# Sliding windows by DMA alone: from two DMA rings to three, with larger copy and store pieces and one more staged batch

## The chip, the cores and the metric

The kernel runs on one core of one Trainium2 chip. The metric is the device time of one execution in microseconds, given as the median of several runs; a profiled execution is taken besides, and all details come from it. The kernel does no arithmetic. It consists of DMA transfers, which the core's 16 DMA engines carry out, and of waits on semaphores.

## The reference

The input `x` has 32 batches of 4096 rows with 256 float32 numbers, 4 MiB a batch. The output takes windows of 64 rows, with a step of 32 rows, so 127 windows a batch, each a plain copy:

```
for i in range(n_windows):            # 127
    start = i * stride                # stride 32
    result[:, i] = x[:, start:start + window_size].copy()   # window 64
```

A window is 64 KB and two neighbours share half of their rows. So nearly every input row is written twice, and the output has 266 MB against an input of 134 MB.

## The kernel before, in words

A batch is seen as 128 blocks of 32 rows (32 KB each). Window w is block w followed by block w + 1. Output batches come about in two ways.

**Copied batches** (20 of 32) go straight from the input to the output in DRAM. `copy` (L93) issues three transfers on the SP queue, of 80, 32 and 15 windows (`COPY_PARTS`, L16). The second number there is how many pieces a 64 KB window is cut into: 16 KB, 32 KB and 16 KB a piece. A piece becomes one DMA packet. Copied data is read twice from the input, since neighbouring windows overlap.

**Staged batches** (12 of 32: 1, 3, ..., 23; `STAGED`, L9) are read once. `load` (L75) brings a batch into one of five tiles in the on-chip memory (`BUFS`, L10), a block on each of 128 partitions. `store` (L83) writes the tile out twice: once as the first halves of the windows, once as the second halves. Both are on the ACT queue, in pieces of 16 KB. Each store covers 128 half windows where a batch has only 127 windows, so the last first-half falls into the next batch's first window, and the first second-half into the previous batch's last window. These halves are garbage there.

So the neighbours of a staged batch must be written after its stores. The order of the copies on SP (`_order`, L102) is this: four `EARLY` batches (L12), which are copied first of all and whose damaged halves are written again at the end (L152 to L158, seven transfers of one 32 KB half each); then batches with no staged neighbour, and the others spread among them, each placed well behind the stores that it waits for (`after_store`, L71, called at L137).

On ACT the order is written out by hand: load 0, load 1, the stores of batch 0, load 2, the stores of batch 1, and so on (L139 to L148). A load into a tile that was used before waits for that tile's stores (L79). At the end SP waits for all stores and copies and clears twelve semaphores one by one (L159 to L163).

Every transfer is issued in `start` (L62), so all DMA lines of the profile carry L62. A queue's transfers lie in a ring per DMA engine; when the ring is full, the issuing instruction lasts until there is room.

Of the kernel before, what the change touches and what calls it, by code (L numbers as in the profile page):

```python
# [1 line left out]

# [4 lines left out]


STAGED = tuple(range(1, 24, 2))  # L9
BUFS = 5  # L10

EARLY = (18, 20, 22, 24)  # L12

BLOCK_PARTS = 2

COPY_PARTS = ((80, 4), (32, 2), (15, 4))  # L16


class _Geometry:


    def __init__(self, x, out, W, S):
        self.B, self.L, self.D = x.shape
        self.x, self.out = x, out
        self.n_win = (self.L - W) // S + 1
        self.n_blk = self.L // S
        self.blk = S * self.D
        self.win = W * self.D
        assert W == 2 * S and self.n_blk == self.n_win + 1 == 128

    def src(self, b, block, dims):

        at = (b * self.n_blk + block) * self.blk
        return bass.AP(self.x.tensor, self.x.offset + at, dims)

    def dst(self, b, half, dims):

        at = b * self.n_win * self.win + half * self.blk
        return bass.AP(self.out.tensor, self.out.offset + at, dims)

    def rows(self, b, w0, n):

        s, d = [[self.blk, n], [1, self.win]], [[self.win, n], [1, self.win]]
        return self.dst(b, 2 * w0, d), self.src(b, w0, s)

    def half(self, b, half, block):

        dims = [[self.blk // 16, 16], [1, self.blk // 16]]
        return self.dst(b, half, dims), self.src(b, block, dims)


class _Kernel:
    def __init__(self, nc, g, tiles):
        self.nc, self.g, self.tiles = nc, g, tiles
        self.loaded = [nc.alloc_semaphore(f"loaded{i}") for i in range(len(tiles))]
        self.stored = [nc.alloc_semaphore(f"stored{i}") for i in range(len(tiles))]
        self.copied = nc.alloc_semaphore("copied")
        self.early = nc.alloc_semaphore("early")
        self.count = {}

    def start(self, engine, out, in_, sem, parts=1):
        engine.dma_start(out=out, in_=in_, max_dma_last_dim=65536 // parts).then_inc(sem, 16)  # L62
        self.count[id(sem)] = self.count.get(id(sem), 0) + 16

    def all_of(self, engine, sem):
        engine.wait_ge(sem, self.count[id(sem)])

    def slot(self, n):
        return divmod(n, len(self.tiles))

    def after_store(self, engine, n):  # L71
        turn, i = self.slot(n)
        engine.wait_ge(self.stored[i], 32 * (turn + 1))

    def load(self, n):  # L75

        g, (_, i) = self.g, self.slot(n)
        if n >= len(self.tiles):
            self.after_store(self.nc.scalar, n - len(self.tiles))  # L79
        src = g.src(STAGED[n], 0, [[g.blk, g.n_blk], [1, g.blk]])  # L80
        self.start(self.nc.scalar, self.tiles[i][:, :], src, self.loaded[i], 2 * BLOCK_PARTS)

    def store(self, n):  # L83

        g, (turn, i) = self.g, self.slot(n)
        self.nc.scalar.wait_ge(self.loaded[i], 16 * (turn + 1))
        for half in (0, -1):
            dst = g.dst(STAGED[n], half, [[g.win, g.n_blk], [1, g.blk]])  # L90
            self.start(self.nc.scalar, dst, self.tiles[i][:, :], self.stored[i], 2 * BLOCK_PARTS)

    def copy(self, b, sem):  # L93

        w = 0
        for rows, parts in COPY_PARTS:
            self.start(self.nc.sync, *self.g.rows(b, w, rows), sem, parts)
            w += rows
        assert w == self.g.n_win


def _order(B):  # L102


    near = {b for s in STAGED for b in (s - 1, s + 1)}
    order = list(EARLY) + [b for b in range(B) if b not in near and b not in STAGED]
    tied = sorted(near - set(EARLY))
    n = len(order) + len(tied)
    for b in tied:
        behind = max(STAGED.index(s) for s in (b - 1, b + 1) if s in STAGED)  # L110
        order.insert(-(-(2 * behind + 5) * n // (2 * len(STAGED))), b)
    return order


@with_exitstack
def kernel(
    ctx: ExitStack,
    tc: tile.TileContext,
    x: bass.AP,
    window_size: bass.AP,  # L120
    stride: bass.AP,
    out: bass.AP,
):
    nc = tc.nc
    W, S = int(window_size), int(stride)
    g = _Geometry(x, out, W, S)
    assert 0 not in STAGED and g.B - 1 not in STAGED
    pool = ctx.enter_context(tc.tile_pool(name="blocks", bufs=1))
    tiles = [pool.tile([g.n_blk, g.blk], x.dtype, name=f"xb{i}") for i in range(BUFS)]

    with tc.tile_critical():
        k = _Kernel(nc, g, tiles)
        for b in _order(g.B):
            if b not in EARLY:
                for s in (b - 1, b + 1):
                    if s in STAGED:
                        k.after_store(nc.sync, STAGED.index(s))  # L137
            k.copy(b, k.early if b in EARLY else k.copied)
        k.load(0)  # L139
        waited = False  # L140
        last = len(STAGED) - 1
        for n, s in enumerate(STAGED):
            if n < last:
                k.load(n + 1)
            if not waited and (s - 1 in EARLY or s + 1 in EARLY):
                k.all_of(nc.scalar, k.early)
                waited = True
            k.store(n)  # L148


        k.all_of(nc.sync, k.early)
        for n, s in enumerate(STAGED):  # L152
            if s - 1 in EARLY or s + 1 in EARLY:
                k.after_store(nc.sync, n)
            if s - 1 in EARLY:
                k.start(nc.sync, *g.half(s - 1, 2 * g.n_win - 1, g.n_blk - 1), k.copied)
            if s + 1 in EARLY:
                k.start(nc.sync, *g.half(s + 1, 0, 0), k.copied)  # L158
        for n in range(len(STAGED)):  # L159
            k.after_store(nc.sync, n)  # L160
        k.all_of(nc.sync, k.copied)
        for sem in [*k.loaded, *k.stored, k.copied, k.early]:
            nc.sync.sem_clear(sem)  # L163


# [1 line left out]
_INS = ['x', 'window_size', 'stride']  # L167
_OUTS = [((32, 127, 64, 256), 'float32')]

_NUMBERS = {'window_size': 64, 'stride': 32}  # L170


# [26 lines left out]
```

## Time and profile before

| | us |
|---|---|
| median of 3 runs (lowest to highest) | 767.51 (767.38 to 767.76) |
| the profiled execution | 768.4 |
| its span, first to last instruction | 766.6 |
| first DMA packet starts, last one ends (from the span's start) | 2.0, 763.8 |
| SP's issue of a copy's three transfers, median from issue to landing | 114.8, 116.7, 97.7 |
| ACT's load, ACT's store, median from issue to landing | 123.2, 84.6 |

The page of this kernel has nothing under the compute engines: GpSimd sets four constants at the start. What counts are the slices of part 2 (busy share of the DMA engines and the rate that they moved data at), the queues of part 3 (q1 is SP's, q10 is ACT's), and the answers on stretches of the span. A row of such an answer gives the stretch, its length, GpSimd's busy time, the clock of the matrix engine (of no matter here), the busy share of the DMA engines and the GB/s.

The long times from issue to landing are time in the ring, behind other transfers.

### The profile page before, as it was taken

How to read it: one execution, taken by the hardware profiler on the slowest of the kernel's cores; microseconds unless marked ns; L12 is line 12 of the kernel's file. 1: busy time of each engine (PE TensorE's matmuls, PEld its weight loads, DVE VectorE, ACT ScalarE, POOL GpSimd, SP SyncE). 2: the span in 40 equal slices, each digit the busy share in tenths (PEclk: the TensorE clock that was granted, in tenths of full speed). 3: DMA queues.
4: the chain of work that ended last, by engine and by line, in shares of the span. 5: the costliest groups of instructions: out<-in, count | busy, mean ns of one | idle time of the engine just before them, and what ended most of it. 6: DMA issues, size and time to landing. Idle time of an engine off the chain costs nothing. (4 is left out here: it accounts for less than half of the span.)

```text
span 766.6 us, 180 instructions
## 1 busy us (share of the span) xinstructions
POOL 0.2 (0%) x4
## 2 busy tenths in 40 slices
POOL 0000000000000000000000000000000000000000
DMA  8999999999999999999999999999999999999996
GB/s 371 425 410 421 405 428 431 408 411 427 423 415 421 431 415 425 432 408 416 427 420 417 431 420 420 423 428 410 414 427 419 422 428 418 417 428 421 420 406 237
DMA packets 19837, 317.70 MB, mean 414 GB/s; under 512 B 1628, under 2 KB 1628, under 8 KB 1740
## 3 DMA queue, kind: packets, MB, share of 16 engines
q1 hardware_dynamic: 10044, 166.70, 51.9%
q10 hardware_dynamic: 9792, 151.00, 47.3%
q14 instruction: 1, 0.01, 0.0%
HBM read 217.02 MB, written 267.35 MB: 632 GB/s over the span
## 5 line engine op out<-in xcount | busy, mean ns | idle before, releaser
L180 POOL MEMSET const-bfloat16-1.0<- 128x1 bf16 x1 | 0.1, 102 | 0.0
L180 POOL MEMSET const-uint8-127<- 128x1 uint8 x1 | 0.1, 102 | 0.0
L180 POOL MEMSET const-float32-0.0<- 128x1 f32 x1 | 0.1, 99 | 0.2 <-issue 0.2
L180 POOL MEMSET const-float32-1.0<- 128x1 f32 x1 | 0.1, 99 | 0.0
## 6 DMA issues: line engine op xcount, KB each, us to landing
out_dram<-in_x_dram SPq DMA_DIRECT2D x20, 5120.0 KB, 114.8
out_dram<-xb ACTq DMA_DIRECT2D x24, 4096.0 KB, 84.6
xb<-in_x_dram ACTq DMA_DIRECT2D x12, 4096.0 KB, 123.2
out_dram<-in_x_dram SPq DMA_DIRECT2D x20, 2048.0 KB, 116.7
out_dram<-in_x_dram SPq DMA_DIRECT2D x20, 960.0 KB, 97.7
out_dram<-in_x_dram SPq DMA_DIRECT2D x7, 32.0 KB, 48.3
```

The costliest lines, as they stand in the source:

```text
L180: nc = _bacc.Bacc("TRN2", target_bir_lowering=False, num_devices=1)
```

## The change

- `STAGED` gets a 13th batch (25), and `EARLY` moves up by two, to 20, 22, 24, 26. There are 19 copied batches left.
- Copies stay on SP. A batch is now two transfers: 112 windows in pieces of 64 KB, and 15 windows in pieces of 16 KB for the first 12 copies, 32 KB for the last 7.
- Stores stay on ACT, in pieces of 32 KB.
- Loads 1 to 12 move to the GpSimd queue, in pieces of 16 KB as before. There they are issued one after the other, the first four without a wait.
- The first load is split by columns into two halves, the first transfer of SP and of ACT, with a semaphore of its own.
- At the end GpSimd, not SP, waits for everything, resets its DMA queue, and clears all semaphores in one instruction.

```
-STAGED = tuple(range(1, 24, 2))
+STAGED = tuple(range(1, 26, 2))
-EARLY = (18, 20, 22, 24)
-BLOCK_PARTS = 2
-COPY_PARTS = ((80, 4), (32, 2), (15, 4))
+EARLY = (20, 22, 24, 26)
+LOAD_PARTS = 2
+REST_PARTS = (4, 2)
+FIRST_COPIES = 12
...
     def load(self, n):
-            self.after_store(self.nc.scalar, n - len(self.tiles))
+            self.after_store(self.nc.gpsimd, n - len(self.tiles))
-        self.start(self.nc.scalar, self.tiles[i][:, :], src, self.loaded[i], 2 * BLOCK_PARTS)
+        self.start(self.nc.gpsimd, self.tiles[i][:, :], src, self.loaded[i], 2 * LOAD_PARTS)
+    def load_first(self):
+        g, n = self.g, self.g.blk // 2
+        for j, engine in enumerate((self.nc.sync, self.nc.scalar)):
+            at = g.src(STAGED[0], 0, [[g.blk, g.n_blk], [1, g.blk]])
+            src = bass.AP(at.tensor, at.offset + j * n, [[g.blk, g.n_blk], [1, n]])
+            self.start(engine, self.tiles[0][:, j * n : (j + 1) * n], src, self.first)
...
     def store(self, n):
-        self.nc.scalar.wait_ge(self.loaded[i], 16 * (turn + 1))
+        if n == 0:
+            self.all_of(self.nc.scalar, self.first)
+        else:
+            self.nc.scalar.wait_ge(self.loaded[i], 16 * (turn + (i > 0)))
         for half in (0, -1):
-            self.start(self.nc.scalar, dst, self.tiles[i][:, :], self.stored[i], 2 * BLOCK_PARTS)
+            self.start(self.nc.scalar, dst, self.tiles[i][:, :], self.stored[i])
-    def copy(self, b, sem):
-        for rows, parts in COPY_PARTS:
-            self.start(self.nc.sync, *self.g.rows(b, w, rows), sem, parts)
+    def copy(self, b, sem, rest_parts):
+        whole = self.g.n_win // 16 * 16
+        self.start(self.nc.sync, *self.g.rows(b, 0, whole), sem)
+        self.start(self.nc.sync, *self.g.rows(b, whole, self.g.n_win - whole), sem, rest_parts)
...
+        k.load_first()
+        for c, b in enumerate(_order(g.B)):
...
+            k.copy(b, k.early if b in EARLY else k.copied, REST_PARTS[c >= FIRST_COPIES])
-        k.load(0)
+        for n in range(1, len(STAGED)):
+            k.load(n)
...
         for n in range(len(STAGED)):
-            k.after_store(nc.sync, n)
-        k.all_of(nc.sync, k.copied)
-        for sem in [*k.loaded, *k.stored, k.copied, k.early]:
-            nc.sync.sem_clear(sem)
+            k.after_store(nc.gpsimd, n)
+        for sem in [*k.loaded, k.first, k.early, k.copied]:
+            k.all_of(nc.gpsimd, sem)
+        nc.gpsimd.dma_reset()
+        used = sorted(sem.num for sem in [*k.loaded, *k.stored, k.first, k.early, k.copied])
+        assert used == list(range(used[0], used[-1] + 1))
+        nc.gpsimd.sem_clear(range(used[0], used[-1] + 1))
```

## The prediction

> **What bounds the kernel now.** No compute engine works here, so the chain of waits is empty and I read the page's slices, then its queues, then the rates in stretches, and last the wait list.
>
> ```profile
> span 766.6 us, 180 instructions
> ...
> DMA  8999999999999999999999999999999999999996
> GB/s 371 425 410 421 405 428 431 408 411 427 423 415 421 431 415 425 432 408 416 427 420 417 431 420 420 423 428 410 414 427 419 422 428 418 417 428 421 420 406 237
> DMA packets 19837, 317.70 MB, mean 414 GB/s; under 512 B 1628, under 2 KB 1628, under 8 KB 1740
> ## 3 DMA queue, kind: packets, MB, share of 16 engines
> q1 hardware_dynamic: 10044, 166.70, 51.9%
> q10 hardware_dynamic: 9792, 151.00, 47.3%
> ...
> HBM read 217.02 MB, written 267.35 MB: 632 GB/s over the span
> ```
>
> The 16 DMA engines are busy from the second slice to the end (51.9% + 47.3% of their span). So time is work on the engines, and only three things move it: bytes, what a byte costs, and the two ends. The second thing varies: slices go from 405 to 432 GB/s at the same busy share. The stretches of the ACT ring (q10) show when. In order: a load, the first store of a pair, the second store, a load, and so on, with copies (q1) always beside them.
>
> ```profile
> 5.00:20.00 15.00, 0.00 (x0) 1.00 1.01 433
> ...
> 84.00:105.00 21.00, 0.00 (x0) 1.00 1.00 409
> 105.00:125.00 20.00, 0.00 (x0) 1.00 1.01 431
> 125.00:146.00 21.00, 0.00 (x0) 1.00 1.01 427
> 146.00:168.00 22.00, 0.00 (x0) 1.00 1.00 398
> 168.00:188.00 20.00, 0.00 (x0) 1.00 1.02 433
> 188.00:209.00 21.00, 0.00 (x0) 1.00 0.99 420
> 209.00:232.00 23.00, 0.00 (x0) 1.00 1.01 410
> ```
>
> The last two columns are the DMA share and GB/s. Loads run at 398 to 410, first stores at 431 to 433, second stores at 420 to 427. The single packets say the same thing (counted in the trace's packet records):
>
> ```
> kind of packet        count   usual ns   mean ns
> copy 16 KB (q1)        7600        611       623
> copy 32 KB (q1)        1280       1213      1253
> load 16 KB (q10)       3072        611       650
> store 16 KB (q10)      6144        611       618
> ```
>
> 611 and 1213 differ by 602, so a packet costs 9 ns and 602 ns per 16 KB; all above that is **stall**. By the same records, stalls take 4.4% of the time of all load stretches, 0.5% of first stores, 2.2% of second stores.
>
> Now the sum of the profiled execution, for one of the 15 engines that carry most (the 15-row pieces leave one engine out, which is why the busy share falls to 0.95 from 725 to 750). A copied batch: 24 x 611 + 4 x 1213 + 27 = 19.54 us; 20 of them, 390.9. A load or store: 16 x 611 + 9 = 9.785; 36 of them, 352.3. The seven 32 KB halves: 0.7. Work 743.8. The first packet starts at 2.0, the last ends at 763.8: stalls are 18.0, which is 2.4% of the work. From there 2.9 us to the span's end: 1.1 until SP sees the last landing, 0.7 for twelve clears, 1.1 of closing barrier. 2.0 + 743.8 + 18.0 + 2.9 = 766.7, the span. The execution itself took 768.4, and the median of the runs is 767.5, 0.9 less; I apply both steps to the result.
>
> **The change, part by part.**
>
> *One more staged batch.* It adds three transfers (29.36) and takes one copied batch (19.54): +9.8 us on every engine. Nothing hides this, because the engines are the bound. In bytes: 317.7 becomes 321.9 MB.
>
> *Bigger pieces.* I take 64 KB at 4 x 602 + 9 = 2417 ns; no such packet is in the trace, so this is an estimate from the two sizes that are. If the 9 ns were charged four times, a 64 KB piece would save nothing. A copy becomes 7 x 2417 + 4 x 611 + 18 = 19.38 (with 2 x 1213 at the end 19.36): 19 of them save 3.3 us together. A store becomes 8 x 1213 + 9 = 9.71: 26 save 1.9. Loads stay at 16 x 611. New work: 368.1 (copies) + 252.5 (stores) + 127.2 (loads) + 0.7 = 748.5, so **+4.7 us net**.
>
> *Three rings.* Engines take one packet from each ring in turn: where 32 KB copies met 16 KB stores, q1's share of the bytes in 5 us pieces rose from 0.50 to between 0.6 and 0.74. So I count bytes per turn, completion packets included: copies 512 KB in 13 packets (39 KB), stores 256 KB in 9 (28), loads 256 KB in 17 (15). That is 48%, 34%, 18% of the bytes. At 431 GB/s: a copied batch per 41 us, a pair of stores per 57, a load per 54. Loads keep just ahead of stores, and 5 tiles give four loads without any wait. Store pair 12 then ends near 20 + 13 x 57 = 761 less what stores gain when loads are through (12 x 54 + 10 = 658), some 10 us; copies end near 12 x 41 + 7 x 37 = 751. The two streams finish together. SP's waits for stores cost nothing as long as its ring holds work: a batch's ring entries fall from 31 to 13, so SP issues about 2.4 times as far ahead. In the present kernel these waits show
>
> ```profile
> SPq L62 <- DMA out_dram<-xb: 61.2, 2, 40.2
> SPq L73 <- DMA out_dram<-xb: 19.2, 3, 9.4
> ```
>
> and the engines stayed full beside them; the last 40.2 is the wait of the late halves at the end.
>
> *GpSimd issues the loads.* Its queue does nothing now but four memsets. Issue time on ACT was 0.4 to 0.6 us a transfer when the ring had room; if GpSimd needs ten times that, it is still 5 of 54 us. If its loads came in smaller packets, at 4 KB say, 768 - 192 more packets x 9 ns = 5 us more work, and loads would fall behind. I take nothing and keep +5.
>
> *First load split.* Both halves lie first in both rings, so all engines load for 9.8 us and store 0 can start near 13 instead of at 43. The engines are full either way: 0 us.
>
> *Stalls.* This is what decides. 48% copies, 18% loads and 34% stores mean reads of 0.66 and writes of 0.82 bytes per byte moved, all the time. Today reads go between 0.52 (stores, stall 0.5% in the clean first ones) and 1.0 (loads, 4.4%). A straight line gives 1.6% at 0.66; if stalls rise only near full reading, it stays at 0.5%. HBM traffic per byte moved also falls, from 1.52 to 1.48. Against it stands the nearest mixture that the trace has: where the ring hands over from loads to stores or back, 2 us pieces with 1 to 35% of loads stall for **8 to 9%**.
>
> ```profile
> 146.00:152.00 6.00, 0.00 (x0) 1.00 0.99 385
> ```
>
> These are some 30 pieces of 2 us, in which engines are also out of step with each other. And with reads of 1.0, 5:20 ran at 433. So neither the read share nor the mixture alone explains a stall. The ends are 0.5% (4 us) and 8% (60 us). By composition the handover row is nearest, but it is a transient; I take the middle of the two steady rows' answers, 1.0% = 7.5 us. This is a choice more than a result.
>
> The Trainium skill speaks against this part: "DMA: Bandwidth & Descriptors", Rules for kernel authors, says that spreading DMAs over SP, ACT and GpSimd does not help bandwidth, since all run on the same 16 engines and only issue time is saved. The trace agrees that both rings share engines (the shares sum to 99%). By that rule alone the stall share stays at 2.4% and the change loses; it says nothing of the order in which reads and writes meet.
>
> *The end.* Today the halves are issued at 755.3 and 756.2, 1.9 and 2.9 us after the last store's packet (753.3), and hide behind copies that run to 763.8. Now 13 stores and 19 copies end together. If stores are last, 2.9 + 0.5 (issue) + 1.1 (issue to first packet, from the start: 0.9 to 2.0) + 0.2 is exposed: +4.7; if copies are last, 0. I take 2.4. One clear on GpSimd for twelve on SP saves 0.65; its reset of the queue is not in the trace: between 0.03 (the shortest GpSimd setup row at the start) and 1.9 (a landing round trip, above). I take 0.2. End: 2.4 us after the last landing's packet.
>
> Sum: 2.0 + 748.5 + 7.5 + 2.4 + 2.4 = 762.8 span, 764.6 as the profiled execution's time, **763.7** as a median.
>
> **Rivals.** A measurement can tell about 0.2%, 1.5 us, from no change; the forecast needs stalls below 9.8 us.
> - *Stalls level out* (forecast, stalls 3 to 9.8): 759 to 766; with the end hidden too, down to 757. For: clean store stretches at 431 to 435, HBM demand a little lower. Chance 0.53.
> - *Break-even* (1.3 to 1.7%): 766 to 769. Chance 0.12.
> - *The stall share stays at 2.4%*, because each kind of packet keeps its own: 18.0 instead of 7.5, **774.2**; slower. Place: all copies and loads, 1 to 650 us. It decides from a stall share of 1.7% on. For: loads stall 6% and copies 2%, and their shares of the bytes hardly change. With smaller load packets besides, 779. Chance 0.22.
> - *The handover state becomes the steady state*: 6 to 8% over 640 us, 38 to 51 us plus the end stretch, 797 to 811. For: the 385 row. Against: 5:20. Chance 0.13.
> - *Nothing changes in the sharing* (rings not by packet): copies then take a third, and run last, alone; that is inside the third case.
>
> **Numbers.** Faster 0.53, same 0.12, slower 0.35. The range takes in the first three cases, 757 to 780, and leaves out the fourth and a part of the third's upper end.
>
> **What would show it.** Right: three queues of 158.3, 109 and 54 MB (the first load's halves lie on SP and ACT); 64 KB packets at 2417 ns; slices without the dips of load stages, at 425 or more up to about 650 us; the last store and last copy within 10 us of each other; stalls of 1%. Wrong: loads' packets not 16 KB, slices at 420 or less throughout (third case), at 400 (fourth), or an empty stretch of the engines while SP or ACT waits.

## The result and the profile after

The change makes the kernel slower, by 1.7%: 780.36 us against 767.48, ratio 1.0169 (95% interval 1.0152 to 1.0187). The forecast was 763.7, with 780 as its upper end. The profiled execution took 780.2 us, its span is 778.4.

The page of the changed kernel, the lines that answer to those of before:

```profile
span 778.4 us, 159 instructions
...
DMA  9999999999999999999999999999999999999994
GB/s 377 418 427 423 400 418 418 444 402 446 391 444 421 436 397 435 413 427 436 411 414 428 439 409 450 392 437 422 431 414 437 398 433 412 422 411 414 414 391 190
DMA packets 11167, 321.95 MB, mean 414 GB/s; under 512 B 1341, under 2 KB 1341, under 8 KB 1453
## 3 DMA queue, kind: packets, MB, share of 16 engines
q1 hardware_dynamic: 4015, 160.47, 49.6%
q10 hardware_dynamic: 3888, 111.15, 33.6%
q0 software_dynamic: 3264, 50.33, 15.3%
HBM read 212.89 MB, written 267.42 MB: 617 GB/s over the span
```

The three queues carry what was foreseen (q0 is GpSimd's). The mean rate is the old 414 GB/s for 4.3 MB more. The slices swing harder than before. A part of that is counting, since a packet's bytes stand where it starts, so the packet records have to say what stalls.

| | before | after | forecast of after |
|---|---|---|---|
| first packet to the last one (after: to the end of the last store's) | 2.0 to 763.8 | 1.9 to 773.8 | |
| work of a busy engine, overlaps taken off | 738.9 | 745.7 | 748.5 (before 743.8) |
| stalls, mean of the engines | 19.3 | 21.3 | 7.5 |
| last engine behind that mean | 3.6 | 4.9 | 0 |
| from there to the span's end | 2.9 | 4.6 | 4.8 |

The overlaps: an engine's next packet starts about 4 ns before the record of the last one ends, which is why the DMA share reads 1.01 in places. A packet costs some 5 ns beyond its bytes, not 9. The rows differ by 6.8 + 2.0 + 1.3 + 1.7 = 11.8 us, the difference of the spans. The span is 15.6 us over its forecast of 762.8: stalls came 13.8 and the last engine 4.9 above what was forecast, work 2.8 and the two ends 0.3 below.

By kind of packet, from the same records: copies stalled 2.2% of their time before and 4.0% after (64 KB packets: 2418 ns as a rule, 2533 in the mean), loads 6.0% before and 1.4% after, stores about 1.2% in both. So the stalls did not stay with their kinds. They moved to the copies. Here is one copied batch in pieces of 4 us (shares of the bytes moved; the stall's share of all engines' time):

```
from   copies  stores  loads   stall
228      0.57    0.29   0.14   0.000
232      0.57    0.27   0.15   0.000
236      0.54    0.31   0.15   0.002
240      0.58    0.28   0.14   0.015
244      0.58    0.27   0.15   0.044
248      0.57    0.29   0.14   0.026
252      0.50    0.32   0.18   0.010
256      0.27    0.40   0.32   0.004
260      0.24    0.53   0.23   0.005
264      0.33    0.50   0.17   0.000
```

For seven packets of 64 KB the copies hold 0.57, for the four packets of 16 KB of the last 15 windows 0.25; the mean is the forecast 0.48. The stall comes late in the high stretch and is gone in the low one. Over the whole run, again in pieces of 4 us, with two kernels from below beside it (the last 40 us of each left out):

```
copies' share   changed kernel     copies in 32 KB (e4)   levelled (e5)
                pieces  stall      pieces  stall          pieces  stall
under 0.40         48   0.002         67   0.001             33   0.004
0.40 to 0.50       15   0.011         65   0.006             59   0.002
0.50 to 0.55       24   0.017         18   0.002             39   0.011
0.55 to 0.60       65   0.030          6   0.004             32   0.007
0.60 to 0.65       16   0.049          2   0.004             10   0.039
0.65 to 0.80       16   0.098          0                      8   0.060
over 0.80           0                 29   0.222              0
```

The share of the moment does not order the stalls by itself: at 0.55 to 0.60 the three kernels stall 3.0%, 0.4% and 0.7%. How long a high stretch has lasted counts too. In pieces of 2 us with a share of 0.53 to 0.65, the changed kernel stalled 1.3% in the first 6 us of a stretch (68 pieces) and 5.3% after that (80 pieces); the levelled one has 64 such early pieces, with 1.0%, and only 8 late ones, again with 5.3%.

A copied byte is read from HBM and written to HBM, so a share c of copies asks for 1 + c bytes of HBM traffic per byte moved. That made **theory A**: reads and writes together have a ceiling, and engines stall while the copies' share of the moment is over what it lets through. **Theory B**: stalls follow the HBM traffic of the whole run, so that a staged batch buys its own work back. **Theory C**: 64 KB packets stall by themselves. "HBM traffic" here is the sum of the page's two figures, read and written; no run shows whether a ceiling on it would sit in HBM or on the way there.

### The profile page after: what moved, and what is told of

It is laid out like the page before. It is cut to its first block, busy times and chain, and to the rows that moved or that the text cites. A ratio compares the mean times of both kernels' runs of the same rounds, so it can differ in the third digit from the quotient of the medians.

```text
span 778.4 us, 159 instructions
## 1 busy us (share of the span) xinstructions
POOL 8.9 (1%) x16
## 4 chain that ended last, share of the span: by engine, by line
another core or an unknown queue 64%; POOL 1%; issue 0%; PEldq 0%
POOL xb L64 1%; PEldq L208 0%
## 5 line engine op out<-in xcount | busy, mean ns | idle before, releaser
L64 POOL DMA_DIRECT2D xb<-in_x_dram x12 | 8.7, 726 | 502.4 <-DMA out_dram<-xb 501.4
```

## The experiments

**e1_twelve**, the changed kernel without the added batch:

```
-STAGED = tuple(range(1, 26, 2))
+STAGED = tuple(range(1, 24, 2))
-EARLY = (20, 22, 24, 26)
+EARLY = (18, 20, 22, 24)
```

> The changed kernel with 12 staged batches instead of 13 (EARLY back to 18, 20, 22, 24); everything else as changed. Each engine has 9.8 us less work. Theory A (an engine stalls when copies hold much of the bytes of the moment, almost not below 45%, 3% at 55 to 60%, 10% above 65%): the turns of the rings stay as they are, so stalls up to 640 us stay; copies are last and alone for some 40 us, which adds 3 to 6 us of stall but hides the late halves (3 us less). 780.4 - 9.8 + 4 - 3 = 771 to 773. Theory B (stalls follow the HBM traffic of the whole run, so that the 13th staged batch buys its own work back): 779 or more. Theory C (64 KB packets stall more by themselves): 770, with the copies' stall share unchanged at 4.6% also in the last 40 us.

Measured: 780.83 us, ratio to before 1.0167 (1.0133 to 1.0200). Work fell by 10.0 us an engine and stalls rose from 21.3 to 33.7. That is theory B's number: here the 13th batch buys its own work back. Of the stalls 22.2 us lie ahead of 640 us (16.9 in the changed kernel; the difference lies in pieces of 4 us with a share above 0.65, 21 of them with 10.0 us of stall against 10 with 4.5; in several of the 21 stores or loads moved next to nothing, and why was not settled) and 5.6 behind 738 us, where stores are through and copies run alone:

```profile
660.00:700.00 40.00, 0.00 (x0) 1.00 1.00 407
700.00:740.00 40.00, 0.00 (x0) 1.00 0.99 399
740.00:760.00 20.00, 0.00 (x0) 1.00 0.94 326
```

The last column, GB/s, drops to 326 with 15 of 16 engines at work all the time.

**e2_before13**, the added batch alone, on the kernel before (`STAGED` to 25 and `EARLY` as in the change):

> The kernel before with a 13th staged batch and nothing else of the change. Theory A: 9.8 us more work (29.36 - 19.54 per engine), a copy share that stays near 50% by the turns of two rings, stalls about as before or 1 us less; some of the late halves' wait (up to 4 us) shows at the end since stores end later: 776 to 781. Theory B: the HBM traffic falls by 4 MB in 484, and stalls by as much as the work grows: 766 to 770.

Measured: 776.92 us, ratio 1.0110 (1.0094 to 1.0126), as theory A said. Work 10.0 us more, stalls 16.8 instead of 19.3. So the added batch alone costs 1.1%, the rest of the change alone 1.7%, and both together 1.7%. On two rings theory B fails, 10.0 us of work for 2.5 us of stall; on three the batch is free. Traffic over the whole run cannot be the rule by itself.

**e3_halved**, all pieces of the changed kernel halved:

```
-LOAD_PARTS = 2
+LOAD_PARTS = 4
-REST_PARTS = (4, 2)
+REST_PARTS = (8, 4)
...
+            self.start(self.nc.scalar, dst, self.tiles[i][:, :], self.stored[i], 4)
...
+        self.start(self.nc.sync, *self.g.rows(b, 0, whole), sem, 2)
```

> The changed kernel with every piece halved: copies 32 KB (the 15 rows 8 and 16 KB), stores 16 KB, loads 8 KB; only the first load's two halves stay at 16 KB. Shares by turn stay 4 to 2 to 1, packets double. Consecutive packets overlap by about 4 ns in the trace, so a packet costs about 5 ns: 700 more packets an engine are 3.5 us. Theory A: the same shares at each moment, the same stalls: 782 to 786. Theory C: the copies' stall share falls from 4.6% to the 2 to 3% that 16 and 32 KB packets had before, 5 to 9 us less: 774 to 779.

Measured: 778.90 us, ratio 1.0141 (1.0122 to 1.0159), just inside theory C's numbers. Stalls are 18.3. By share they are as in the changed kernel at 0.55 to 0.60 (0.030) and lower above 0.65 (0.063 against 0.098). So by one profile of each the size of a packet has a part of some 3 us, where the ceiling is passed furthest; it does not remove the stalls.

**e4_copy32**, the copies alone cut smaller:

```
-REST_PARTS = (4, 2)
+REST_PARTS = (2, 2)
...
+        self.start(self.nc.sync, *self.g.rows(b, 0, whole), sem, 2)
```

> The changed kernel with copies cut to 32 KB (the 15 rows too), stores 32 KB and loads 16 KB as changed. Copies get 40% of the bytes by turn, so staged batches end early, near 635 us, and copies run the last 115 us alone. Theory A: almost no stall up to 550 us (under 1%, against 2.6% now), all of the stall at the end, where copies alone must show what they stall by themselves, 10% or more: 12 us and up; the late halves are hidden. 765 to 775, and a trace with 430 GB/s and more up to 550 us, 390 or less behind 640. Theory C: copies' stall share near 3% throughout, not piled up at the end; 770.

Measured: 792.35 us, ratio 1.0312 (1.0295 to 1.0330). Theory A had the place right and the size wrong. Its stretches:

```profile
20.00:200.00 180.00, 2.14 (x3) 1.00 1.00 429
200.00:400.00 200.00, 2.85 (x4) 1.00 1.00 433
400.00:550.00 150.00, 0.71 (x1) 1.00 1.00 432
550.00:640.00 90.00, 0.00 (x0) 1.00 1.01 429
640.00:660.00 20.00, 0.00 (x0) 1.00 1.01 341
660.00:760.00 100.00, 0.00 (x0) 1.00 0.98 326
```

For 640 us, at a copies' share of 0.4, the engines run with 3.7 us of stall in all; then copies alone stall 22% of the time at 326 GB/s, and 29.3 us of stall pile up there. The expectation had put copies alone at a stall of 10% or more, 390 GB/s or less.

**e8_copies64**, no staging at all, to measure the ceiling by itself (all 32 batches copied by SP, `COPY_PARTS = ((112, 1), (15, 1))`, no loads, stores or waits on them):

> No staging at all: SP copies all 32 batches in 64 KB pieces, everything else left out (the output is complete). It measures the ceiling by itself. Theory A: the rate is that of the end of the run with 32 KB copies, 326 GB/s, that is 652 GB/s of reads and writes: 266.3 MB take 815 us. Theory C (64 KB pieces worse than 32 KB): under 310 GB/s, over 860 us.

Measured: 817.69 us, one execution. Its page:

```profile
DMA  9999999999999999999999999999999999999996
GB/s 309 347 321 309 354 315 328 337 312 328 341 325 337 315 341 328 334 321 321 347 321 318 337 321 344 325 334 328 315 341 325 334 325 325 331 328 328 331 321 260
...
HBM read 266.34 MB, written 266.34 MB: 653 GB/s over the span
```

The engines are full from end to end and move 327 GB/s; the last line is the ceiling, **653 GB/s of reads and writes**. It is the rate of 32 KB copies alone, so 64 KB is no worse here, against theory C. With unstalled engines at 432 GB/s, 432 x (1 + c) = 653 gives c = 0.51; at 0.667 (64 KB copies beside 32 KB stores, no loads) the ceiling allows 653 / 1.667 = 392. The changed kernel's pieces above 0.65 moved about 390, and the stretch in which it ran at 0.667 steadily, with loads through, moved 396:

```profile
672.00:688.00 16.00, 0.00 (x0) 1.00 1.00 396
```

A ceiling of copies by themselves does not explain this stretch: two thirds of 396 are 264, well under the 327 that copies reach alone.

**e5_level** spreads the copies in time. Same bytes, same 13 batches, no more data packets:

```
-        whole = self.g.n_win // 16 * 16
-        self.start(self.nc.sync, *self.g.rows(b, 0, whole), sem)
-        self.start(self.nc.sync, *self.g.rows(b, whole, self.g.n_win - whole), sem, rest_parts)
+        w = 0
+        for rows, parts in ((32, 1), (32, 1), (32, 1), (16, 1), (15, 1)):
+            self.start(self.nc.sync, *self.g.rows(b, w, rows), sem, parts)
+            w += rows
```

> The changed kernel with each copied batch cut into transfers of 32, 32, 32, 16 and 15 windows, all in 64 KB pieces (before: 112 in 64 KB, 15 in smaller ones). The same bytes, 13 staged, no more packets. By turns the copies still hold 57% while they have a packet, but a completion entry now falls after every one or two packets, where it came after seven. Theory A, sharpened by the last runs (reads and writes together cannot pass about 650 GB/s for long, and a copied byte counts twice, so the copies' share must not stay above 0.5): no long stretch at 0.57 or more, stalls fall from 21 us to 10 to 16, and copies end last and hide the late halves: 765 to 773. Theory C (64 KB packets stall by themselves): the same 4.6% on copies, 778 or more.

Measured: 766.04 us, ratio 0.9997 (0.9976 to 1.0018): the loss is gone. Stalls are 11.5. Stretches of it:

```profile
200.00:400.00 200.00, 2.86 (x4) 1.00 1.01 432
400.00:640.00 240.00, 1.43 (x2) 1.00 1.00 432
640.00:740.00 100.00, 0.00 (x0) 1.00 1.00 416
740.00:754.00 14.00, 0.00 (x0) 1.00 0.96 333
```

and the same stretches of the changed kernel:

```profile
200.00:400.00 200.00, 2.86 (x4) 1.00 1.00 424
400.00:640.00 240.00, 1.43 (x2) 1.00 1.00 423
640.00:740.00 100.00, 0.00 (x0) 1.00 0.99 413
```

432 against 424 while three rings run. The copies' share by turns is that of the changed kernel's first 12 copies, 0.48: 13 ring entries for 512 KB in both. Its spread in time differs, and the last 15 windows are now 64 KB pieces, which the next run takes alone. It is not a matter of which addresses a long transfer spreads over, since e4 kept the transfers of 112 windows and hardly stalled for 640 us. What is left to lose is behind 640 us: loads are through, copies hold 0.6 and more, and from 740 they are alone.

**e10_rest64** tells whether it was the cutting or the small pieces of the 15 windows, which went as well:

```
-REST_PARTS = (4, 2)
+REST_PARTS = (1, 1)
```

> The changed kernel with one edit: the 15 windows too in 64 KB pieces, still one transfer of 112 and one of 15. It tells whether the small pieces of the 15 windows made the levelled kernel better by going, or the cutting into short transfers. Theory A: eight 64 KB packets in a row instead of seven and no low stretch between them, so the ceiling is hit more: stalls 21 us or more, 776 to 785. Rival D (the mix of sizes within a batch makes the stalls): near the levelled kernel, 766 to 770.

Measured: 782.64 us, ratio 1.0205 (1.0190 to 1.0220). So the small pieces going did not do it; that leaves the cutting. Without the low stretch between, stalls grow to 23.8; here the copies' share by turns is also higher, 0.54.

**e6_level_lead**, the second staged batch loaded at the start too (each of SP and ACT issues a half of batches 0 and 1; GpSimd starts at batch 2):

> The kernel of the run before with the second staged batch, too, loaded at the start by SP and ACT in two halves, so that loads stay a whole batch ahead and ACT need not wait for a load between two pairs of stores. Theory A: the stretches in which stores are missing and copies hold 0.65 to 0.75 go; 2 to 5 us less than the run before. If those stretches cost nothing, the same within 1 us, or up to 4 us more since loads end earlier and copies are left with stores alone for longer.

Measured: 769.49 us, ratio 1.0044 (1.0023 to 1.0064), at the upper end of its second case (about 3.5 us more than the run before). Loads were through at 586 us instead of 659, and the copies met stores alone for longer.

**e7_two32**, larger pieces on the two old rings (`BLOCK_PARTS = 1`, `COPY_PARTS = ((112, 2), (15, 2))`):

> The kernel before (two rings, 12 staged) with larger pieces alone: copies, loads and stores all in 32 KB. 560 packets an engine fewer at about 5 ns are 2.7 us less work; the copies' share by turn is 0.50 where it was 0.52. Theory A: stalls no more than before: 762 to 766. Theory C: stalls 3% and more on copies throughout, 768 to 772.

Measured: 771.50 us, ratio 1.0063 (1.0046 to 1.0081), in theory C's numbers. But the expectation had left out that staged batches now end early, at 716 us:

```profile
20.00:716.00 696.00, 0.00 (x0) 1.00 1.00 424
716.00:750.00 34.00, 0.00 (x0) 1.00 0.94 325
```

8.0 of its 23.3 us of stall lie in that end, where copies are alone. Up to there it ran at 424, where the kernel before ran at 419 to 422.

**e9_late32** moves copies from the end, where they are too many, to the middle (lines against the changed kernel):

```
...
+        level = ((48, 1), (32, 1), (32, 1), (15, 1))
+        for rows, parts in level if rest_parts == 4 else ((112, 2), (15, 2)):
...
-FIRST_COPIES = 12
+FIRST_COPIES = 16
```

> The levelled kernel with the copies' share moved in time: the first 16 copied batches in transfers of 48, 32, 32 and 15 windows of 64 KB pieces (0.50 by turns instead of 0.475), the last 3 in 32 KB pieces, since by then loads are through and 64 KB beside 32 KB stores would be 0.67. Theory A: no copies alone at the end, stalls 8 to 11 us instead of 11.5, and less at the end: 760 to 765. If the ceiling has nothing to do with it (only the number of transfers matters), 766 or more.

Measured: 763.93 us, ratio 0.9965 (0.9952 to 0.9978): 0.35% faster than the kernel before, and faster than the changed one. Against the levelled kernel the two intervals just touch. Stalls 9.1; from 640 to 740 it moves 424 GB/s and from 740 to 754 351, where the levelled one had 416 and 333.

**e11_late32_12**, the same with 12 staged batches (and the last 3 of 20 copies in 32 KB):

> The levelled kernel with late 32 KB copies, but 12 staged batches (EARLY 18, 20, 22, 24; the last 3 of 20 copies in 32 KB). It tells whether the 13th batch, 9.8 us of work, is worth having once shares are level. Theory A: the copied share of all bytes is 0.52, over what the ceiling lets through, and here the copies run some 45 us alone at the end at 326 GB/s: stalls grow by as much as the work falls, 763 to 769. If stalls stay at 9 us: 754 to 756.

Measured: 765.02 us, ratio 0.9971 (0.9955 to 0.9987). Work 10.0 us less, stalls 18.3 instead of 9.1, of which 9.3 behind 700 us. Twelve or thirteen makes no difference that can be told here: a little under the ceiling one pays in engine work, a little over it in stalls.

## Why the prediction was wrong

- **The step that failed** is "Stalls": "mean reads of 0.66 and writes of 0.82 bytes per byte moved, all the time". The mean was right and "all the time" was not. One transfer of 112 windows puts seven 64 KB packets in a row on each engine, and while they last the copies hold 0.57, about 30 us, then 0.25 for 10 us. A stall that starts only above a ceiling depends on the high stretches, and the mean hides them. A high stretch of 6 us costs little, one of 30 us stalls 5% from its seventh microsecond on. 21.3 us came instead of 7.5; levelling the same work (e5) brought 11.5, so about 10 of the 14 us missed lie there. Of e5's 11.5 us, 6.3 lie behind 640 us, where copies hold 0.6 and more.
- **The variable was wrong as well.** I ordered stalls by the share of reads, since load stages stalled most. On three rings it is reads plus writes, with a ceiling of 653 GB/s (e8). The trace before had signs of it: copies alone at its end stalled 11% (752 to 756), and pieces with a share above 0.6 stalled 4 to 5%. I had counted 1.52 bytes of HBM traffic per byte moved; at 431 GB/s that is 655, the ceiling itself. But the ceiling is not the whole of it on two rings. In the kernel before, pieces of 4 us with a copies' share of 0.45 to 0.55 ask for the same traffic whatever is beside the copies; 78 of them without loads stalled 0.9%, and 42 with loads at 0.4 or more of the bytes stalled 3.4%, some 5.7 of the 19.3 us. There the order by reads held, and its cause stays open; with three rings loads never held so much for long.
- **The handover row** (385 GB/s) was nearer to the truth than the middle that I chose, but not for the reason given. Mixing loads and stores was harmless at a copies' share of 0.4: e4 does it for 550 us with 2.8 us of stall. What made the handover rows of the kernel before stall was not tried.
- **The rival that came nearest**, "the stall share stays at 2.4%" (774.2), was near in time but not by its mechanism: each kind was to keep its toll, and loads went from 6.0% to 1.4% while copies went from 2.2% to 4.0%.
- **Work**: +4.7 was +6.8, because a packet's fixed cost is 5 ns and not 9, so larger pieces saved less. The 2417 ns for 64 KB was right (2418).
- **The end** was right in its number, 4.6 us from the last store packet to the span's end for a forecast of 4.8, but by luck. The forecast took the middle, 2.4, between stores last (4.7) and copies last (0), and 2.4 after it. Stores were last, 773.8, so its own working would have given 7.1. The last halves were issued 0.7 and 1.2 us behind the last store packet (774.5 and 775.0), not 1.9 and 2.9, and were written at 776.7, which exposed 2.9 us; 1.7 followed. GpSimd's reset took 0.3 us, its clear 0.1.
- **Three rings by turns** was right, with completion entries included. That GpSimd's issue and the split first load cost nothing fits the trace, though no run takes either out: GpSimd needed 0.72 us a load, its ring was never the last, and the engines were full from the first slice to the last but one.
- SP waited far longer than before without harm, as the forecast said:

```profile
SPq L75 <- DMA out_dram<-xb: 509.6, 9, 69.2
SPq L64 <- DMA out_dram<-xb: 230.7, 4, 85.8
```

## What to carry to other kernels

When a transfer engine is full and something behind it has a ceiling, look at the mix of the moment and not at the mean: bins of a few microseconds, ordered by the suspected load, showed in one table what slices of 19 us had hidden. How a transfer is cut decides how rings interleave, so a copy that both reads and writes HBM should be issued in short transfers that spread it evenly; here one long transfer bunched it. And measure the ceiling alone early: one run of pure copies gave the number that the whole forecast lacked.

## What was not expected of the hardware

- Copies from HBM to HBM alone keep all engines occupied and move 327 GB/s, 653 GB/s of reads and writes. The Trainium skill, "HBM Reference", Specifications (TRN2), has about 716 GB/s a domain. No run here moved that with its one core over its span, and none shows what sets the 653.
- A completion entry takes a turn of its ring, though its packet lasts 9 ns. The order of the packets shows it: when e5's packets are put in line by engine (each starts some 4 ns before the last one's record ends), between 50 and 600 us a completion of SP's ring is followed by a packet of ACT's ring in 1056 of 1073 cases and by one of its own in 10. The shares say the same: in e5 the 12 loads on GpSimd's ring were through at 659 us. With completions counted as turns loads get 15.1 of 82.9 KB, 78 GB/s at 432, and 50.3 MB need 640 us; without them 16 of 112 KB would be 62 GB/s and over 800 us. This is what levels the copies. It works the other way too: ahead of 640 us the changed kernel's pieces of 4 us with a copies' share above 0.65 hold 8.0 completions of stores in the mean, the other pieces 1.7, so there the stores lose a turn on many engines at once.
- At the same share of 0.57 the first 10 to 15 us of a high stretch run without stalls (228 to 240 above). Over the whole run it sets in sooner on average, after some 6 us (above). What takes up the excess until then was not tried and stays open.
